# The first layer's gate product as seven block products of half size, with sums of weights on GpSimd

## The chip, the cores and the metric

The kernel runs on one core of a Trainium2 chip. What counts is the device time of one execution in microseconds. An engine's name stands as in the profile: PE is TensorE (PEld its weight loads), DVE is VectorE, ACT is ScalarE, POOL is GpSimd, SP is SyncE, which issues nearly all transfers.

## What is computed

Two layers act on 1024 tokens of width 1024. Each layer is a mixer, an MLP and a gated per-layer embedding (PLE). The change is in the first layer's PLE and in the end of the MLP before it:

```python
gate = jax.nn.sigmoid(rms_norm(h, ln_ple[layer]) @ w_ple_gate[layer])   # 1024x1024 @ 1024x1024
h = h + (p[layer] @ w_ple_proj[layer]) * gate                           # 1024x256 @ 256x1024
```

All is float32.

## The kernel before

**Products.** A float32 operand is split in two parts, `hi` and `lo` (`split`, line 229: ScalarE copies `hi` with rounding, VectorE subtracts it). A product is three matmuls (`mm3`): hi·hi, hi·lo, lo·hi, added up in PSUM. Activations lie with the features on the partitions, in `acc[m][h]`: 8 tiles `m` of 128 features, 2 halves `h` of 512 tokens. Weights are the stationary operand (128x128), activations the moving one (128x512).

**Normalisation.** `put_h` writes gain times `acc` as hi and lo without the row scale. The scale `rb[h]` (one over the root mean square of each token) comes from a sum of squares (`add_square`), which `rms` adds over the partitions with small matmuls against a column of ones; GpSimd takes the power. With `far=True` the scale is written to DRAM and read back to all partitions; both transfers are issued by SyncE, which takes its queue in order.

**The PLE.** `ple` loops over the two token halves, over four pieces of 256 columns of the gate's weight and over the two tiles in each. Each of the 16 results is one sum over 8 tiles in PSUM, 24 matmuls. `close` follows one result behind: it multiplies by `rb`, takes tanh, makes the projection `pp` (six matmuls) in an `aux` bank, combines and adds into `acc`, stores `acc` in `h_dram`, and adds its square. After a half, `put_h` makes the next stage's operands. The gate's weight is thus loaded and split twice.

**Buffers.** Raw weights have 8 buffers (`RB`), split weights 12 (`WB`, six pairs). `tmp` has 4. The slots `c0` to `c13`, `A0` to `A5` and `B` are reused by name. PSUM has 8 banks: tags `mm`, `tr`, `aux`, `sc`, two each. `mm_ps` takes tags in turn from `T.wide`.

**Order.** The instructions of each engine run in a fixed order. The context that builds the program plans it with modelled times (`schedule_with_timeline_sim=True`), by the order of the text where several could go; waits come from what an instruction reads and writes. So a step's place in its engine's queue is planned, and its time is not.

**Around the change.** The MLP's second product ends with `product2(2)` and `product2(4)`, whose sums `add` puts into `acc`. Behind the PLE comes `attention`: projections of v and of the first head's q and k, half 0 first. Its weights are split with the low parts on GpSimd. The MLP and the second layer's PLE (`ple_out`) already use seven block products, with sums of weights on VectorE.

Of the kernel before, what the change touches and what calls it, by code (L numbers as in the profile page):

```python
# [11 lines left out]
F32 = mybir.dt.float32  # L12
F32R = mybir.dt.float32r
# [5 lines left out]
P = 128  # L19
D = 1024  # L20
S = 1024
KT = D // P
# [21 lines left out]
def f32(ap):  # L44
    return ap.bitcast(F32)
# [73 lines left out]
class Trunk:  # L119
# [54 lines left out]
    def raw(self, n, m):  # L174
        return self.wp.tile([P, n, m], F32, tag="raw", name=self.nm("raw"), bufs=RB)

    def parts(self, raw, lo_engine):
        hi, lo = (self.wp.tile(list(raw.shape), F32R, tag="w", name=self.nm("w"), bufs=WB) for _ in range(2))
        self.split(raw, hi, lo, lo_engine)

        self.low_mark = self.split_mark
        return hi, lo
# [63 lines left out]
        nc.vector.scalar_tensor_tensor(lo, h, gain, f32(hi), ALU.mult, ALU.subtract)  # L246
        self.hs_new[half][k] = (hi, lo)

    def add_square(self, half, h):
        nc = self.nc  # L250
        if self.sqs[half] is None:
            self.sqs[half] = self.sp.tile([P, HT], F32, tag=f"sqs{half}", name=self.nm("sqs"), bufs=1)
            nc.scalar.activation(self.sqs[half], h, AF.Square)
        else:
            sq = self.tmp()
            nc.scalar.activation(sq, h, AF.Square)
            nc.vector.tensor_tensor(self.sqs[half], self.sqs[half], sq, ALU.add)

    def take_hs(self, half, ms=None, rows=True, far=False):

# [36 lines left out]
    def mlp(self, x, x_tags, gain, w1, w2, gain_next, h_dram, p, last):  # L297
# [319 lines left out]
        if last:  # L617
            product2(4, y, True)
            add(4, 1, y, put)
            x = [self.mm_ps() for _ in range(4)]  # L620
            product2(2, x, True, rms)
            self.mlp_mark = self.pe.mark
            add(0, 1, x, square)
        else:
            product2(2, y, True)
            add(0, 1, y, put)
            product2(4, x, False, rms)
            self.mlp_mark = self.pe.mark
            add(4, 1, x, put)
        self.hs[1] = self.hs_new[1]  # L630
        return acc, pT

# [25 lines left out]
        return hi, lo  # L658


    def ple(self, pT, acc, wg, wpj, gain_next, h_dram):
        nc = self.nc
        gates = []

        def close():
            h, m, ps = gates.pop(0)
            pp = self.aux_ps()
            for k in range(2):
                self.mm3(pp, [x[:, k, (m % 2) * P : (m % 2 + 1) * P] for x in wq[m // 2]], pT[h][k], k == 0, k == 1)
            t = self.tmp()  # L670
            nc.vector.tensor_tensor(t, ps, rb[h], ALU.mult)
            nc.scalar.activation(t, t, AF.Tanh, scale=0.5)
            t2 = self.tmp()
            nc.vector.scalar_tensor_tensor(t2, t, 1.0, pp, ALU.add, ALU.mult)
            nc.vector.scalar_tensor_tensor(acc[m][h], t2, 0.5, acc[m][h], ALU.mult, ALU.add)
            nc.sync.dma_start(h_dram[m, :, h * HT : (h + 1) * HT], acc[m][h])
            self.add_square(h, acc[m][h])

        hs, rb, sqs = list(self.hs), list(self.rb), self.sqs[1]
        self.new_hs()  # L680
        for h in range(2):
            for j in range(4):
                w = self.weight(wg[:, j * 256 : (j + 1) * 256], KT, 256)
                for ml in range(2):
                    m = 2 * j + ml
                    ps = self.mm_ps()
                    for k in range(KT):
                        self.mm3(ps, w.at(k, slice(ml * P, (ml + 1) * P)), hs[h][k], k == 0, k == KT - 1)
                    n = KT * h + m
                    if n == 0:  # L690
                        wq = [self.weight_p(wpj, i) for i in range(4)]
                    if n == 2:
                        rb[1] = self.rms(1, sqs, far=True)[1]
                    while len(gates) > (n < 3):
                        close()
                    gates.append((h, m, ps))
            close()
            for m in range(KT):
                self.put_h(m, h, acc[m][h], gain_next[:, m : m + 1])
            self.take_hs(h, rows=False)  # L700

# [1390 lines left out]
def trunk(tc, x, p, ln_mix_e, w_in_e, gmlp_v_gain, gmlp_ws, gmlp_bs, gdn_conv, gdn_a_log, gdn_dt_bias, gdn_out_gain,  # L2092
          w_out_e, ln_mix_o, w_qkv_o, attn_q_gain, attn_k_gain, diff_lambda, attn_sub_gain, w_out_o, ln_mlp, w_mlp1,
          w_mlp2, ln_ple, w_ple_gate, w_ple_proj, masks, out):
    with ExitStack() as ctx:
# [55 lines left out]
        for layer in range(2):  # L2151
            T.wide = ("mm", "tr")
            accs = [None] * 4

            def acc_of(m, h):
                i = 2 * h + m // 4
                if accs[i] is None:
                    accs[i] = T.slot(f"A{i}", [P, 4, HT], F32, "acc")
                return accs[i][:, m % 4]


            if layer:
# [12 lines left out]
            T.ple(pT, acc, w_ple_gate[0], w_ple_proj[0], gain[3], h_dram)  # L2175
            T.wide = ("mm",)
            T.attention(w_qkv_o[0], w_out_o[0], gain[4], h_dram)

# [40 lines left out]
```

## Time and profile before

| | us |
|---|---|
| median of 3 runs | 2503.58 (2502.16 to 2503.97) |
| profiled execution | 2502.4 |
| its span, first to last instruction | 2500.7 |
| PE busy in the span | 2490.9 |
| DVE busy | 1809.6 |
| ACT busy | 1312.8 |
| POOL busy | 284.0 |

In the rows of a timeline stand start, length, engine, line, operation, tiles (out<-in), shape, number, and in brackets the idle time before with what ended it. In a row of groups stand the number, the busy time, the mean length of one in ns, and the idle time before. Matmuls overlap, so their lengths are longer than the distance between two. In a row of waits: who waited, for whom, us in total, times, longest.

### The profile page before, as it was taken

Reading aid. Unit: us, or ns where it says so; the run is one execution under the profiler, and the core shown is the slowest. Engines: PE = TensorE matmul, PEld = TensorE weight load, DVE = VectorE, ACT = ScalarE, POOL = GpSimd, SP = SyncE. Lnnn points to the kernel's source line nnn. Section 1 sums busy time; section 2 is a strip of 40 time slices with the busy share of each in tenths; the row PEclk is TensorE's granted clock in tenths of the full one; section 3 lists DMA queues with packets and bytes.
Section 4 is the critical chain, followed back from the end, with each engine's and each line's share of the span. In section 5 each row is a group of like instructions: output and inputs, shape, how many; then the busy total and the mean of one; then the engine's idle time right before and its main releaser. Section 6 shows DMA issues by size and latency. Waiting matters only on the chain.

```text
span 2500.7 us, 39891 instructions
## 1 busy us (share of the span) xinstructions
PE 2490.9 (100%) x13905; PEld 2138.7 (86%) x13905; DVE 1809.6 (72%) x3542; ACT 1312.8 (52%) x2669; POOL 284.0 (11%) x267
## 2 busy tenths in 40 slices
PE   9999999999999999999999999999999999999999
PEld 7898998888888888888999999988888888888887
DVE  7868665787666887656577877776887666787586
ACT  6635473555555444544466666654654555445452
POOL 0211220000000000000444444410000000000000
PEclk9999999999999999999999999999999999999999
DMA  8464435467548756544211111367466548566651
GB/s 238 128 185 106 145 127 183 139 208 245 178 169 276 241 164 208 188 130 132 80 54 58 52 52 60 102 206 234 157 220 224 193 161 299 197 192 200 197 177 64
DMA packets 318834, 410.81 MB, mean 164 GB/s; under 512 B 45764, under 2 KB 181928, under 8 KB 318632
## 3 DMA queue, kind: packets, MB, share of 16 engines
q1 hardware_dynamic: 318072, 407.73, 50.9%
q8 instruction: 109, 1.79, 0.3%
q14 instruction: 93, 0.76, 0.1%
q10 hardware_dynamic: 560, 0.53, 0.1%
HBM read 295.95 MB, written 112.20 MB: 163 GB/s over the span
## 4 chain that ended last, share of the span: by engine, by line
PE 96%; DVE 2%; DMA 1%; issue 0%; ACT 0%; POOL 0%; SPq 0%; ACTq 0%; DVEq 0%
PE mm L80 83%; PE po L80 3%; PE qk L80 2%; PE aux L80 2%; PE tr L83 2%; DMA x<-in_x_dram 1%; DMA raw<-in_w_in_e_dram 0%; DVE lg L1128 0%; PE pks L80 0%; PE pkq L80 0%; PE pkk L80 0%; PE pvn L80 0%; PE pgm L80 0%; PE pab L83 0%; PE pst L80 0%
## 5 line engine op out<-in xcount | busy, mean ns | idle before, releaser
L230 ACT CAST w<-raw 128x512 fp32r<-128x512 f32 x598 | 366.5, 617 | 472.4 <-PE mm L80 410.2
L80 PE MATMUL mm<-g,w 128*128 128x512 f32 x2592 | 601.0, 394 | 0.0
L80 PEld LDWEIGHTS mm<-g,w 128*128 128x128 f32 x2592 | 486.9, 188 | 113.0
L80 PE MATMUL mm<-hi,w 128*128 128x512 f32 x1728 | 554.6, 396 | 0.1
L234 DVE TENSOR_TENSOR w<-raw,w 128x512 fp32r<-128x512 f32 x534 | 368.1, 696 | 199.3 <-ACT w L230 189.9
L80 PE MATMUL mm<-w,hi 128*128 128x256 f32 (+2 forms) x2528 | 507.4, 295 | 0.5 <-DVE k L1030 0.5
L80 PEld LDWEIGHTS mm<-w,hi 128*128 128x128 f32 x2528 | 401.2, 188 | 13.4 <-issue 0.7
L80 PEld LDWEIGHTS mm<-hi,w 128*128 128x128 f32 x1728 | 324.4, 188 | 74.7 <-DVE w L234 0.8
L80 PE MATMUL mm<-w,lo 128*128 128x256 f32 (+2 forms) x1264 | 370.2, 294 | 0.0
L80 PE MATMUL mm<-lo,w 128*128 128x512 f32 x864 | 340.3, 394 | 0.0
L80 PE MATMUL mm<-t,w 128*128 128x512 f32 x1152 | 271.2, 394 | 0.0
L80 PEld LDWEIGHTS mm<-t,w 128*128 128x128 f32 x1152 | 216.4, 188 | 50.5
L80 PEld LDWEIGHTS mm<-w,lo 128*128 128x128 f32 x1264 | 238.2, 189 | 5.5
L80 PEld LDWEIGHTS mm<-lo,w 128*128 128x128 f32 x864 | 162.5, 188 | 36.0
L275 POOL TENSOR_TENSOR r<-ms,mhalf 128x4 f32<-128x4 f32 x12 | 13.7, 1139 | 1512.3 <-DVE ms L273 1483.2
L234 DVE TENSOR_TENSOR g<-graw,g 128x512 fp32r<-128x512 f32 x216 | 148.0, 687 | 5.9 <-DMA gd<-g 5.0
L230 ACT CAST g<-graw 128x512 fp32r<-128x512 f32 x216 | 132.7, 617 | 22.7 <-DMA gd<-g 10.9
L1131 ACT ACTIVATE lg<-lg,nm 128x128 f32<-128x128 f32 (+7 forms) x128 | 99.2, 776 | 64.8 <-DVE nm L1128 62.9
L370 ACT ACTIVATE g<-g 128x512 f32<-128x512 f32 x100 | 63.0, 630 | 81.4 <-DVE g L304 81.0
L1128 DVE CUSTOM_DVE_ANT_0 lg<-qk,al 128x512 f32<-128x512 f32 (+3 forms) x128 | 74.4, 589 | 37.6 <-PE qk L80 33.6
L234 POOL TENSOR_TENSOR w<-raw,w 128x512 fp32r<-128x512 f32 x64 | 85.1, 1348 | 76.3 <-ACT w L230 51.5
L80 PE MATMUL mm<-ohi,w 128*128 128x512 f32 x256 | 83.6, 398 | 0.5 <-DVE t L1310 0.4
(360 smaller groups left out, 3573.9 us busy)
## 6 DMA issues: line engine op xcount, KB each, us to landing
raw<-in_w_mlp_dram SPq DMA_DIRECT2D x352, 256.0 KB, 3.4
graw<-gd SPq DMA_DIRECT2D x224, 256.0 KB, 2.8
gd<-g SPq DMA_DIRECT2D x192, 256.0 KB, 3.4
raw<-in_w_ple_gate_dram SPq DMA_DIRECT2D x76, 256.0 KB, 3.5
acc<-h_dram SPq DMA_DIRECT2D x64, 256.0 KB, 4.5
keep<-in_w_mlp_dram SPq DMA_DIRECT2D x64, 256.0 KB, 4.4
raw<-in_w_in_e_dram SPq DMA_DIRECT2D x60, 256.0 KB, 4.0
h_dram<-acc SPq DMA_DIRECT2D x48, 256.0 KB, 2.8
```

The lines of the kernel that those rows point to most:

```text
L80: self._next(self.engine.matmul(*a, **k))
L83: self._next(self.engine.transpose(*a, **k))
L230: inst = self.nc.scalar.copy(hi, src)
L234: inst = (lo_engine or self.nc.vector).tensor_tensor(lo, src, f32(hi), ALU.subtract)
L275: nc.gpsimd.tensor_tensor(r, ms, self.mhalf[:, 0:4], ALU.pow)
L370: nc.scalar.activation(g, src, AF.Relu)
L1128: nc.vector.tensor_tensor_reduce(out=lg[:, k0:k1], in0=ps[:, : k1 - k0], in1=al[:, u0 + k0 : u0 + k1], scale=-1.0, scalar=3.0e38 if c == 0 ...
L1131: nc.scalar.activation(lg[:, :n], lg[:, :n], AF.Exp, bias=nm[:, r, nch - 1 : nch], scale=-1.0, accum_out=me.sums[:, b, r : r + 1])
```

## The change

The gate product becomes seven products of half size (Strassen's scheme in Winograd's form). The weight is cut in four blocks by halves of outputs (`i`) and inputs (`j`), the activations by halves of features and tokens. Each block product is 4 x 4 tile products over 512 tokens. In the order of the text they are numbered 1 to 7. Products 1, 4, 5 and 6 (`chain`) are added up in the same four PSUM banks `x`, which are read after each of them. Products 2, 3 and 7 (`single`) go tile by tile through other banks. The sums of weights (`sum1`, `sum3`, `sum4`) are made on GpSimd; one of them goes to DRAM (`s2_dram`) and is read twice. One product has its weight's low part on GpSimd. The sums of activations (`t1` to `t4`) are made with the gain on VectorE and ScalarE; `t1` beside the MLP's last product, and the MLP no longer makes `put`'s operands for half 1. The additions of squares go to GpSimd. `close` runs for four results at a time, with products 2 and 7 and after products 5 and 6, and the projection's weights are loaded in two parts.

```diff
-    def add_square(self, half, h):
+    def add_square(self, half, h, eng=None):
...
-            nc.vector.tensor_tensor(self.sqs[half], self.sqs[half], sq, ALU.add)
+            (eng or nc.vector).tensor_tensor(self.sqs[half], self.sqs[half], sq, ALU.add)
...
             product2(2, y, True)
-            add(0, 1, y, put)
-            product2(4, x, False, rms)
+            add(0, 1, y, square)
+            t1 = self.hs_new[1]
+
+            def make_t1():
+                for k in range(4):
+                    z = self.scaled(self.tmp(), acc[k][0], gain_next[:, k : k + 1])
+                    nc.vector.scalar_tensor_tensor(z, acc[k][1], gain_next[:, k : k + 1], z, ALU.mult, ALU.subtract)
+                    t1[k] = self.split(z, *self.hs_parts(1, k))
+
+            product2(4, x, False, {**rms, 9: make_t1})
             self.mlp_mark = self.pe.mark
-            add(4, 1, x, put)
+            add(4, 1, x, lambda m, h: self.add_square(h, acc[m][h], nc.gpsimd))
...
+    def ple(self, pT, acc, gain, wg, wpj, gain_next, h_dram):
+        hs, rb, sqs = list(self.hs), list(self.rb), self.sqs[1]
+        b11, b21, t1 = hs[0][0:4], hs[0][4:], hs[1][0:4]
+        self.new_hs()
+        s2_dram = self.dp.tile([4, P, HT], F32, name="s2_dram")
...
+        def raw(i, j, k):
+            t = self.raw(1, HT)[:, 0]
+            nc.sync.dma_start(t, wg[(4 * j + k) * P : (4 * j + k + 1) * P, i * HT : (i + 1) * HT])
+            return t
...
+        def left(src, eng=nc.vector):
+            hi, lo = (self.wp.tile([P, 1, HT], F32R, tag="w", name=self.nm("w"), bufs=WB)[:, 0] for _ in range(2))
+            return self.split(src, hi, lo, eng)
...
+        def chain(ps, make, b, new=False):
+            for k in R:
+                a = make(k)
+                for q in R:
+                    one(ps[q], a, b[k], q, k, new and k == 0, k == 3, not new)
+
+        def single(a, b, tags, done):
+            for q in R:
+                ps = self.aux([P, HT], tags[q], "mm")
+                for k in R:
+                    one(ps, a[k], b[k], q, k, k == 0, k == 3, False)
+                done(q, ps)
+
+        def close(l, h, q, ps, plus, wp):
+            m = 4 * l + q
+            t = self.tmp()
+            if plus is not None:
+                tt(t, ps, plus, ALU.add)
+                ps = t
+            tt(t, ps, rb[h], ALU.mult)
+            nc.scalar.activation(t, t, AF.Tanh, scale=0.5)
             pp = self.aux_ps()
             for k in range(2):
+                self.mm3(pp, [x[:, q * P : (q + 1) * P] for x in wp[k]], pT[h][k], k == 0, k == 1)
+            nc.vector.scalar_tensor_tensor(t, t, 1.0, pp, ALU.add, ALU.mult)
+            a = stt(acc[m][h], t, 0.5, acc[m][h], ALU.add)
+            nc.sync.dma_start(h_dram[m, :, h * HT : (h + 1) * HT], a)
+            self.add_square(h, a, nc.gpsimd)
...
+        x = [self.mm_ps() for _ in R]
+        chain(x, lambda k: left(raw(0, 0, k)), b11, True)
+        a12 = [left(raw(0, 1, k)) for k in R]
+        u0 = f32_tiles((6, 7, 8, 9), "u")
+        for q in R:
+            nc.scalar.copy(u0[q], x[q])
...
+        for k in R:
+            self.scaled(t3[k], acc[k][1], g(k))
+            stt(t3[k], acc[4 + k][1], g(4 + k), t3[k], ALU.subtract)
+            stt(t2[k], acc[k][0], g(k), t3[k], ALU.add)
+        rb[1] = self.rms(1, sqs, far=True)[1]
+        single(a12, b21, ("sc",) * 4, lambda q, ps: close(0, 0, q, ps, u0[q], wp0))
+
+        def sum1(k):
+            a21, a22, a11 = raw(1, 0, k), raw(1, 1, k), raw(0, 0, k)
+            tt(a21, a21, a22, ALU.add, nc.gpsimd)
+            tt(a11, a21, a11, ALU.subtract, nc.gpsimd)
+            nc.sync.dma_start(s2_dram[k], a11)
+            return left(a21)
+
+        p5 = f32_tiles((6, 7, 8, 9), "p5")
+        s1 = [sum1(k) for k in R]
+        t2s = parts(t2, (0, 0))
+        single(s1, t1, ("sc",) * 4, lambda q, ps: nc.scalar.copy(p5[q], ps))
+        t3s = parts(t3, (0, 4))
+        b22 = put(1, 1, (1, 4), gain)
+        for k in R:
+            stt(t2[k], acc[4 + k][0], g(4 + k), t2[k], ALU.subtract)
+        chain(x, lambda k: left(sum2(k), nc.vector), t2s)
+        u = f32_tiles((10, 11, 12, 13), "u")
+        for q in R:
+            nc.scalar.copy(u[q], x[q])
+        t4s = parts(t2, (1, 0))
+
+        def sum3(k):
+            a11, a21 = raw(0, 0, k), raw(1, 0, k)
+            return left(tt(a11, a11, a21, ALU.subtract, nc.gpsimd), nc.vector)
+
+        chain(x, sum3, t3s)
+        wp1 = weight_p(1, [self.slot(f"c{i}", [P, HT], F32R, "wp") for i in range(4)])
+        for q in R:
+            close(1, 1, q, x[q], p5[q], wp1)
+        put_next(0, 0, (0, 0))
+        chain(x, lambda k: left(raw(1, 1, k), nc.gpsimd), t4s)
+        for q in R:
+            tt(u[q], u[q], p5[q], ALU.add, nc.gpsimd)
+        for q in R:
+            close(1, 0, q, x[q], None, wp1)
+
+        def sum4(k):
+            a12, s2 = raw(0, 1, k), sum2(k)
+            return left(tt(a12, a12, s2, ALU.subtract, nc.gpsimd), nc.vector)
+
+        put_next(1, 0, (1, 0))
+        single([sum4(k) for k in R], b22, ("sc", "sc", "tr", "tr"), lambda q, ps: close(0, 1, q, ps, u[q], wp0))
+        self.take_hs(0, rows=False)
+        put_next(1, 1, (0, 4))
+        put_next(0, 1, (1, 4))
+        self.take_hs(1, rows=False)
```

`sum2(k)` reads one saved sum back from `s2_dram` into a raw buffer; `parts` splits four activations; `put` and `put_next` are `put_h` for four tiles into given places.

More of the change, by code (lines that the diff above doesn't have):

```diff
@@ L667, in close @@
             pp = self.aux_ps()
             for k in range(2):
[L669 to L700, printed above, removed]
+                self.mm3(pp, [x[:, q * P : (q + 1) * P] for x in wp[k]], pT[h][k], k == 0, k == 1)
@@ new lines, in close, with put @@
+            nc.vector.scalar_tensor_tensor(t, t, 1.0, pp, ALU.add, ALU.mult)
+            a = stt(acc[m][h], t, 0.5, acc[m][h], ALU.add)
+            nc.sync.dma_start(h_dram[m, :, h * HT : (h + 1) * HT], a)
+            self.add_square(h, a, nc.gpsimd)
+        def put(l, h, place, by):
+            new = []
+            for q in R:
+                m = 4 * l + q
+                hi, lo = self.hs_parts(place[0], place[1] + q)
+                self.scaled(hi, acc[m][h], by[:, m : m + 1])
+                stt(lo, acc[m][h], by[:, m : m + 1], f32(hi), ALU.subtract)
+                new.append((hi, lo))
+            return new
@@ new lines, in put_next, with parts @@
+        def put_next(l, h, place):
+            self.hs_new[h][4 * l : 4 * l + 4] = put(l, h, place, gain_next)
+        def parts(srcs, place):
+            return [self.split(s, *self.hs_parts(place[0], place[1] + k)) for k, s in enumerate(srcs)]
+        x = [self.mm_ps() for _ in R]
[4 more added lines that the diff above has]
+            nc.scalar.copy(u0[q], x[q])
@@ L2174, in trunk @@
                 break
-            T.ple(pT, acc, w_ple_gate[0], w_ple_proj[0], gain[3], h_dram)
+            T.ple(pT, acc, gain[2], w_ple_gate[0], w_ple_proj[0], gain[3], h_dram)
             T.wide = ("mm",)
```

35 lines of the change are left out of this document (31 added, 4 removed).

## The prediction

> **What bounds the kernel now.** I read the page first: the engines, then the chain that ended last.
>
> ```profile
> span 2500.7 us, 39891 instructions
> PE 2490.9 (100%) x13905; PEld 2138.7 (86%) x13905; DVE 1809.6 (72%) x3542; ACT 1312.8 (52%) x2669; POOL 284.0 (11%) x267
> PE 96%; DVE 2%; DMA 1%; issue 0%; ACT 0%; POOL 0%; SPq 0%; ACTq 0%; DVEq 0%
> ```
>
> TensorE is the bound, and the last chain is nearly all matmul. Averages say nothing of this stage, so I cut the first layer's PLE out with the timeline and asked for busy times by window.
>
> ```profile
> 1091.50 0.40 PE L80 MATMUL mm<-hi,w 128*128 128x512 f32 x1
> ...
> 1204.16 0.39 PE L80 MATMUL aux<-phi,wpl 128*128 128x512 f32 x1
> 1204.39 0.40 PE L80 MATMUL mm<-w,hi 128*128 128x256 f32 x2
> ...
> 1213.01 0.95 PE L80 MATMUL aux<-ones,sqs 128*128 128x1 f32 x8
> ```
>
> ```profile
> core 0: us, PE busy (x) PEld busy (x) DVE busy (x) ACT busy (x) POOL busy (x), PEclk, DMA share, GB/s
> 1091.50:1204.39 112.89, 112.89 (x497) 92.04 (x496) 73.02 (x114) 50.44 (x87) 8.37 (x7) 1.00 0.38 119
> ...
> 2420.00:2450.00 30.00, 30.00 (x135) 24.43 (x134) 29.56 (x48) 17.40 (x32) 0.00 (x0) 1.00 0.17 57
> ```
>
> The PLE runs from 1091.50 to 1204.39, and TensorE has no gap in it, at clock 1.00. So a matmul taken out is worth its full pitch, and every wait that is put in is paid in full. VectorE has 39.9 us free, ScalarE 62, GpSimd 104. The last row is the second layer's PLE, which already has seven products with the sums on VectorE: there VectorE is busy 29.56 of 30.00 us and TensorE still has no gap. A full VectorE alone is thus no loss; a late one is. Now the groups of the stage.
>
> ```profile
> L80 PE MATMUL mm<-hi,w 128*128 128x512 f32 x256 | 82.1, 394 | 0.0
> L80 PE MATMUL mm<-lo,w 128*128 128x512 f32 x128 | 50.5, 394 | 0.0
> L230 ACT CAST w<-raw 128x512 fp32r<-128x512 f32 x33 | 20.1, 614 | 29.4 <-PE mm L80 25.3 <-DMA raw<-in_w_ple_gate_dram 3.9
> L234 DVE TENSOR_TENSOR w<-raw,w 128x512 fp32r<-128x512 f32 x27 | 18.4, 690 | 6.9 <-ACT w L230 6.6
> L80 PE MATMUL aux<-phi,wph 128*128 128x512 f32 x32 | 12.8, 399 | 0.0
> L257 DVE TENSOR_TENSOR sqs<-sqs,t 128x512 f32<-128x512 f32 x16 | 11.0, 688 | 0.6 <-ACT t L256 0.2
> L674 DVE SCALAR_TENSOR_TENSOR t<-t,aux 128x512 f32<-128x512 f32 x15 | 10.3, 686 | 24.2 <-PE aux L80 24.1
> L80 PE MATMUL aux<-ones,sqs 128*128 128x1 f32 x16 | 1.9, 239 | 0.0
> ```
>
> **Matmuls.** The gate product is 384 matmuls of 128x512 (256 + 128). The projection adds 96 (32, and twice more through the two other terms of `mm3`). Two sums of squares take 1.9 us. The pitch is (112.89 - 1.9) / 480 = 0.231 us; the 394 ns of one overlaps its neighbours and is not the price. Seven block products of 4 x 4 tile products, three matmuls each, are 7 x 48 = 336. The projection stays at 16 x 6. So 48 go: 48 x 0.231 = **11.1 us less**, and the stage becomes 101.8 us if TensorE never waits. Sums in PSUM cost no matmul: the chained products only clear the start flag.
>
> **Loads.** Instead of 32 pieces of the gate's weight come 44 and four reads of a saved sum; four sums are stored. That is 20 transfers of 256 KB more, 5 MB on some 13 MB (119 GB/s x 112.89 us), with the DMA engines 0.38 busy.
>
> ```profile
> raw<-in_w_ple_gate_dram SPq DMA_DIRECT2D x76, 256.0 KB, 3.5
> ...
> ACT w L230 <- DMA raw<-in_w_ple_gate_dram: 3.9, 1, 3.9
> ...
> SPq L281 <- DMA rd<-r: 16.8, 2, 8.5
> ```
>
> The whole stage waited for a weight once, 3.9 us on ScalarE, with eight raw buffers covering it. What threatens is the queue: SyncE waits up to 8.5 us in `rms(far=True)` for the row scale to come back, and what is behind it stands. In the new order that wait falls behind product 1 (some 14 to 23 us into the stage). Queued behind it are stores of the saved sums and perhaps the last pieces for product 3. These sums are read for product 4, at 40 us; the pieces are wanted at 31. A load issued at 23, 3.5 us to landing, 1.3 of sum (GpSimd's rows below) and 1.3 of split (0.61 and 0.69) is ready at 29. I take nothing, with 3 us as the upper end.
>
> **VectorE and GpSimd.** Counted from the diff, VectorE has these 128x512 operations from the first matmul on: 28 splits of weights less the 4 of product 1 that come earlier and 4 given to GpSimd, 4 splits of the projection, 12 of activations, 16 combinations with the gain (t2, t3, b22, t4), 60 in `close` (12 have the added sum, 48 the rest), 16 `put`: 128, where the window's row counts 114. The additions of squares go to GpSimd, which also gets 16 sums, 4 low parts and 4 additions of u and p5; with the four squares at the end of the MLP it has 42 (two of the PLE's squares are plain writes by ScalarE). The rows that price both lie at the end of the stage, where GpSimd already splits attention weights.
>
> ```profile
> 1198.27 1.35 POOL L234 TENSOR_TENSOR w<-raw,w 128x512 fp32r<-128x512 f32 x1 [8.59 <-ACT w L230]
> 1200.54 1.43 POOL L234 TENSOR_TENSOR w<-raw,w 128x512 fp32r<-128x512 f32 x1 [0.91 <-ACT w L230]
> 1203.42 3.29 POOL L234 TENSOR_TENSOR w<-raw,w 128x512 fp32r<-128x512 f32 x2 [1.46 <-ACT w L230]
> ...
> 1215.31 5.04 POOL L234 TENSOR_TENSOR w<-raw,w 128x512 fp32r<-128x512 f32 x4
> ```
>
> ```profile
> 1197.71 0.75 DVE L246 SCALAR_TENSOR_TENSOR lo<-acc,cols,hi 128x512 fp32r<-128x512 f32 x1
> 1198.38 0.68 DVE L671 TENSOR_TENSOR t<-mm,rb 128x512 f32<-128x512 f32 x1
> 1198.98 1.19 DVE L246 SCALAR_TENSOR_TENSOR lo<-acc,cols,hi 128x512 fp32r<-128x512 f32 x1
> 1200.10 0.68 DVE L257 TENSOR_TENSOR sqs<-sqs,t 128x512 f32<-128x512 f32 x1
> 1200.70 3.13 DVE L246 SCALAR_TENSOR_TENSOR lo<-acc,cols,hi 128x512 fp32r<-128x512 f32 x3
> 1203.76 0.68 DVE L674 SCALAR_TENSOR_TENSOR t<-t,aux 128x512 f32<-128x512 f32 x1
> 1204.36 1.19 DVE L246 SCALAR_TENSOR_TENSOR lo<-acc,cols,hi 128x512 fp32r<-128x512 f32 x1
> 1205.47 1.79 DVE L675 SCALAR_TENSOR_TENSOR acc<-t,acc 128x512 f32<-128x512 f32 x1
> ...
> 1211.35 0.69 DVE L257 TENSOR_TENSOR sqs<-sqs,t 128x512 f32<-128x512 f32 x1 [0.70 <-ACT t L256]
> ```
>
> Starts 1197.71, 1198.38 and 1198.98 give VectorE's pitch: 0.67 us with a gain column, 0.60 without. Thirty-two have one: 32 x 0.67 + 96 x 0.60 = 79 us of 101.8, which fits. An undisturbed GpSimd operation is 5.04 / 4 = 1.26 us, so its 42 are 53 us, which fits too. But the rows also show the two in each other's way. With GpSimd at work, an operation with two SBUF inputs takes 1.19 or 1.79 us instead of 0.75 and 0.69, and three take 3.13 instead of some 2.09; the two that read PSUM (`mm`, `aux`) keep 0.68. The loss is 0.44 + 1.04 + 0.44 + 1.10 = 3.0 us for four GpSimd operations, 0.76 each; GpSimd loses 6.07 - 5.04 = 1.0 us. Of VectorE's 128 only 32 read PSUM (12 additions, 4 multiplications, 16 with the projection). At 0.76 the 42 cost 32 us: 79 + 32 = 111, over 101.8. So VectorE will be late in places.
>
> [...]
>
> Where does lateness reach TensorE? I laid the new order out from 0 at the first matmul: product 1 to 11; sum of squares; product 2 with its four closings to 29; product 3 to 40; the two middle chained products to 62; closings to 68; product 6 to 79; closings to 84; product 7 with closings to 101.8. From 40 to 62 VectorE has about 14 operations (9 us): lateness is made up there, and those GpSimd operations cost nothing. Three places have little cover:
> - At 29. Of the 12 `w` buffers, product 2 holds 8 to its last quarter, so two of product 3's four splits start 2 us before it ends and are wanted 3 us after. In product 2 VectorE has 24 operations, 15 us, and some 11 of GpSimd (8 us): 23 in 17, less a lead of about 3. Slack after the split itself is 3.6. Cost 0 to 3, taken as 1.
> - At 79. Four banks are finished together; the third projection needs an `aux` buffer that VectorE frees by the first closing, about half a microsecond ahead. Lateness of 1 to 2 us comes through: 0 to 5, taken as 1. The same at 62, but VectorE arrives rested.
> - The end. Before, the last square ended at 1212.04 and TensorE's sum of squares stood at 1213.01 between attention matmuls, 8.6 us past the stage. Its place in the new order is planned; where VectorE or GpSimd is later than planned, TensorE stands there: 0 to 6, taken as 1. Half 1 itself is read later still.
>
> Tags `mm` and `tr`, taken four at once, need two banks of the MLP's last sums, 1.4 us later than the first two: nothing. ScalarE gets twelve copies from PSUM and some twenty scalings; with 50.44 of 112.89 us busy it hides them; without that cover they would cost at most their length at the same three places. The four t1 operands go beside the MLP's last product, where four `put`s leave: nothing.
>
> **Sum.** 2502.4 (profiled execution) - 11.1 + 3 = 2494.3. The median stands 1.2 above that execution, so the forecast is **2495.5**.
>
> **The rivals.** (a) VectorE's lateness is half absorbed: the 3.6 us of slack at 29 and the half microsecond at 79 go to a backlog near the computed 111 - 101.8 = 9 us. Waits of 9 us give 2503.6 - 11.1 + 9 = 2501.5, no difference. For it: the sum of 111. Against: 22 us in the middle are idle. (b) Slower: two-input operations and GpSimd exclude each other for whole instructions, and VectorE becomes the bound. Each of 42 costs it 1.26, so 79 + 53 = 132 us; 8 of that may run past the stage, as in the trace (1204.39 to 1212.04); waits are 132 - 8 - 101.8 = 22 us: 2503.6 - 11.1 + 22 = 2514.5. Its place is the closings from 62 on and the end. It decides slower from 16 us of waits, (16 + 101.8 + 8 - 79) / 42 = 1.1 us for each GpSimd operation, against 0.76 seen. For it: 1.79 and 3.13. Against: those rows stand in a stretch without idle VectorE time. (c) SyncE's waits hold product 3's weights: 3 to 5 us more on the forecast, about 2499.5. Against: the stage's single wait of 3.9. (d) All is hidden: 2492.5. That the matmuls do not go can't be: their count follows from the loops.
>
> **How the numbers follow.** A measurement of this kernel can tell 0.2%, 5 us, from no change: 2498.6 and 2508.6. Forecast (waits to 6 us) with (d): 0.50. (a) and (c): 0.22, of which 0.04 still lands below 2498.6. (b), from 2508.6 on: 0.28. Faster 0.54, same 0.18, slower 0.28. The forecast's own range is 2492 to 2498.5; to leave no more than 2 in 10 out the range goes to 2512.
>
> **What would show it.** Right: 432 matmuls of 128x512 in the stage at the same pitch, TensorE's gaps together about 3 us, at product 3's start, in the closings after product 6, at the last sum of squares, each released by VectorE or GpSimd; 128x512 operations of two SBUF inputs stretched to 1.2 to 1.9 us. Wrong: gaps over 11 us, a longer pitch or clock below 1.00, or gaps released by a DMA.

## The result, and the profile after

| | before | after |
|---|---|---|
| median of 6 runs, us | 2503.18 (2502.16 to 2503.97) | 2514.04 (2511.77 to 2516.18) |
| profiled execution, us | 2502.4 | 2515.1 |
| its span, us | 2500.7 | 2513.3 |

The kernel became slower: the ratio is 1.0042 with a 95% interval of 1.0031 to 1.0053. The forecast of 2495.5 us was wrong in its sign, and 2514.04 lies above its range.

The page after, with the same lines as were read before:

```profile
PE 2491.7 (99%) x13857; PEld 2136.2 (85%) x13857; DVE 1846.4 (73%) x3556; ACT 1327.5 (53%) x2697; POOL 351.2 (14%) x309
PE 93%; DVE 4%; issue 1%; DMA 1%; ACT 1%; POOL 0%; SPq 0%; DVEq 0%; ACTq 0%; POOLq 0%
```

13905 - 13857 = 48 matmuls are gone, as counted. The last chain now runs over VectorE for 4% instead of 2%. How much of this belongs to the stage is told by an instruction that both kernels have behind it, the first `qk` matmul of the attention. The busy times from the first matmul of the PLE to that instruction, before:

```profile
1091.50:1244.77 153.27, 153.27 (x841) 132.41 (x840) 91.40 (x144) 65.17 (x114) 28.64 (x25) 1.00 0.34 106
```

The row of after, and below it the stage in parts (columns as in the prediction's windows: PE, PEld, DVE, ACT, POOL, granted clock, DMA share, GB/s):

```profile
1091.38:1253.56 162.18, 150.96 (x792) 127.70 (x791) 127.32 (x157) 74.59 (x133) 96.21 (x69) 0.96 0.41 127
...
1100.00:1110.00 10.00, 6.75 (x28) 5.52 (x27) 10.00 (x7) 1.86 (x4) 9.92 (x7) 0.83 0.34 113
1110.00:1120.00 10.00, 7.94 (x25) 5.79 (x24) 10.00 (x15) 3.11 (x6) 2.82 (x3) 0.66 0.47 151
1120.00:1180.00 60.00, 59.98 (x259) 48.30 (x259) 49.53 (x61) 31.64 (x56) 31.41 (x22) 1.00 0.55 163
1180.00:1224.00 44.00, 38.76 (x221) 32.44 (x219) 39.04 (x46) 22.50 (x41) 27.50 (x20) 1.00 0.31 102
1224.00:1230.00 6.00, 5.35 (x32) 5.27 (x33) 0.55 (x4) 1.08 (x3) 5.50 (x5) 0.72 0.49 138
```

The stretch takes 162.18 us instead of 153.27, 8.9 more, where 11.1 less were expected: **20.0 us are lost in it**. TensorE stands for 162.18 - 150.96 = 11.2 us. The other 8.8 are in its busy time: 150.96, where 153.27 - 11.1 = 142.2 would do. The clock column names a part of that, 0.83, 0.66 and 0.72 in three rows where it was 1.00 before. From the `qk` matmul to the end it is 2513.3 - 1253.56 = 1259.7 us, where it was 2500.7 - 1244.77 = 1255.9: 3.8 more are lost behind the stage.

The loss has two places, the stage's start and its end. From 1120 to 1180 TensorE has no gap and VectorE is idle for 10.5 of 60 us: the middle is as forecast. Before it, from 1100 to 1120, VectorE is busy without a pause (10.00 and 10.00) and TensorE is not. Who released TensorE tells the view of its waits, 1085 to 1250:

```profile
PE aux L80 <- DVE t L751: 3.7, 4, 1.6
PE mm L80 <- DVE w L234: 3.3, 2, 2.1
PE aux L80 <- POOL sqs L257: 3.2, 1, 3.2
PE mm L80 <- POOL w L234: 0.6, 1, 0.6
PE mm L80 <- ACT v L1178: 0.3, 1, 0.3
```

No DMA is among them. But for 0.3 us, for which an attention matmul waits for ScalarE, all are VectorE's or GpSimd's. TensorE's timeline shows the places:

```profile
1103.71 0.40 PE L80 MATMUL mm<-hi,w 128*128 128x512 f32 x1
1107.35 1.87 PE L80 MATMUL aux<-ones,sqs 128*128 128x1 f32 x8 [3.25 <-POOL sqs L257]
...
1110.08 0.63 PE L80 MATMUL aux<-phi,wp 128*128 128x512 f32 x1
1110.51 0.63 PE L80 MATMUL aux<-plo,wp 128*128 128x512 f32 x1
1113.19 1.22 PE L80 MATMUL mm<-hi,w 128*128 128x512 f32 x2 [2.06 <-DVE w L234]
...
1204.74 0.50 PE L80 MATMUL aux<-phi,wp 128*128 128x512 f32 x1 [1.63 <-DVE t L751]
```

The longest gap is where product 1 ends, 13 us into the stage: the sum of squares for the row scale waits 3.25 us for GpSimd. A few matmuls later a weight of product 2 is not split yet, 2.06 us. Of the others, 1.24 us is a split for product 7, and 1.63 and 1.33 us are closings of product 7; the rest are below 0.7 us each. After the first gap two matmuls stand 1110.51 - 1110.08 = 0.43 us apart, nearly twice the 0.231 of before.

Why are both engines late there? VectorE's timeline of after, in the first stretch:

```profile
1097.61 1.78 DVE L691 SCALAR_TENSOR_TENSOR lo<-acc,cols,hi 128x512 fp32r<-128x512 f32 x1
1099.31 1.79 DVE L234 TENSOR_TENSOR w<-raw,w 128x512 fp32r<-128x512 f32 x1
1101.03 3.48 DVE L691 SCALAR_TENSOR_TENSOR t<-acc,cols,t 128x512 f32<-128x512 f32 x2
...
1112.46 0.68 DVE L234 TENSOR_TENSOR w<-raw,w 128x512 fp32r<-128x512 f32 x1
```

and GpSimd's:

```profile
1091.80 3.01 POOL L687 TENSOR_TENSOR raw<-raw,raw 128x512 f32<-128x512 f32 x2 [26.24 <-DVE w L234]
...
1097.09 1.75 POOL L257 TENSOR_TENSOR sqs<-sqs,t 128x512 f32<-128x512 f32 x1
1098.80 1.75 POOL L687 TENSOR_TENSOR raw<-raw,raw 128x512 f32<-128x512 f32 x1
1100.51 1.74 POOL L257 TENSOR_TENSOR sqs<-sqs,t 128x512 f32<-128x512 f32 x1
...
1107.26 3.40 POOL L687 TENSOR_TENSOR raw<-raw,raw 128x512 f32<-128x512 f32 x2
```

The two engines go in step, one operation of each in 1.71 us (1097.09, 1098.80, 1100.51 on one, 1097.61, 1099.31, 1101.03 on the other). Alone a split takes VectorE 0.68 us, as at 1112.46, when GpSimd is done. From 1091.80 to 1110.66 GpSimd has eleven such operations, seven of the eight first sums of weights and the four squares of the MLP's end, beside product 1 and the gap behind it. And the groups of the stage (1091.38 to 1224), for VectorE and for GpSimd:

```profile
L691 DVE SCALAR_TENSOR_TENSOR lo<-acc,cols,hi 128x512 fp32r<-128x512 f32 x20 | 30.2, 1513 | 4.2 <-ACT hi L670 4.1
L234 DVE TENSOR_TENSOR w<-raw,w 128x512 fp32r<-128x512 f32 x20 | 19.7, 984 | 9.3 <-ACT w L230 9.3
L691 DVE SCALAR_TENSOR_TENSOR acc<-t,acc 128x512 f32<-128x512 f32 x16 | 16.2, 1014 | 0.4
L691 DVE SCALAR_TENSOR_TENSOR t<-acc,cols,t 128x512 f32<-128x512 f32 x12 | 13.4, 1131 | 0.0
L751 DVE SCALAR_TENSOR_TENSOR t<-t,aux 128x512 f32<-128x512 f32 x16 | 10.8, 676 | 0.8 <-ACT t L747 0.7
L687 DVE TENSOR_TENSOR t<-t,rb 128x512 f32<-128x512 f32 x12 | 10.5, 877 | 0.3
```

```profile
L257 POOL TENSOR_TENSOR sqs<-sqs,t 128x512 f32<-128x512 f32 x18 | 27.8, 1542 | 22.2 <-ACT t L256 22.1
L687 POOL TENSOR_TENSOR raw<-raw,raw 128x512 f32<-128x512 f32 x16 | 24.5, 1535 | 45.9 <-DVE w L234 26.2 <-DMA raw<-in_w_ple_gate_dram 17.7 <-DMA raw<-s_dram 1.5
```

Against 750 ns with a gain column and 690 ns without, the operations with two SBUF inputs lose 20 x 0.763 + 20 x 0.294 + 16 x 0.324 + 12 x 0.381 + 12 x 0.187 = 33.2 us; the one that reads PSUM (`aux`) loses nothing (676 ns, 686 before). GpSimd has 49 operations of this size in that window: 18 squares, 16 sums, 4 additions of `u` and `p5`, and 11 low parts of weights.

### The profile page after: what moved, and what is told of

Its sections match the earlier page's. It is cut to its first block, busy times and chain, and to the rows that moved or that the text cites. A ratio compares the mean times of both kernels' runs of the same rounds, so it can differ in the third digit from the quotient of the medians.

```text
span 2513.3 us, 39935 instructions
## 1 busy us (share of the span) xinstructions
PE 2491.7 (99%) x13857; PEld 2136.2 (85%) x13857; DVE 1846.4 (73%) x3556; ACT 1327.5 (53%) x2697; POOL 351.2 (14%) x309
## 3 DMA queue, kind: packets, MB, share of 16 engines
q8 instruction: 109, 1.79, 0.3%
## 4 chain that ended last, share of the span: by engine, by line
PE 93%; DVE 4%; issue 1%; DMA 1%; ACT 1%; POOL 0%; SPq 0%; DVEq 0%; ACTq 0%; POOLq 0%
PE mm L80 80%; PE po L80 3%; PE qk L80 2%; PE tr L83 2%; PE aux L80 2%; DVE acc L691 0%; DMA rd<-r 0%; DVE lo L691 0%; DVE t L691 0%; DVE lg L1261 0%; PE aux L83 0%; DMA raw<-in_w_ple_gate_dram 0%; DVE w L234 0%; DVE t L751 0%; PE pks L80 0%
## 5 line engine op out<-in xcount | busy, mean ns | idle before, releaser
L230 ACT CAST w<-raw 128x512 fp32r<-128x512 f32 (+1 forms) x594 | 363.5, 618 | 431.2 <-PE mm L80 378.1
L80 PE MATMUL mm<-hi,w 128*128 128x512 f32 x1696 | 545.7, 397 | 3.3 <-DVE w L234 3.3
L234 DVE TENSOR_TENSOR w<-raw,w 128x512 fp32r<-128x512 f32 (+1 forms) x526 | 365.5, 701 | 192.8 <-ACT w L230 184.4
L80 PEld LDWEIGHTS mm<-hi,w 128*128 128x128 f32 x1696 | 318.9, 188 | 77.7 <-DVE w L234 4.9
L80 PE MATMUL mm<-lo,w 128*128 128x512 f32 x848 | 334.4, 395 | 0.0
L234 DVE TENSOR_TENSOR g<-graw,g 128x512 fp32r<-128x512 f32 x216 | 147.6, 685 | 5.3 <-DMA gd<-g 4.2
L1264 ACT ACTIVATE lg<-lg,nm 128x256 f32<-128x256 f32 (+7 forms) x128 | 99.2, 775 | 70.3 <-DVE nm L1261 68.4
L234 POOL TENSOR_TENSOR w<-raw,w 128x512 fp32r<-128x512 f32 x68 | 91.5, 1366 | 42.5 <-ACT w L230 24.1
```

What stands on the lines that cost most here:

```text
L80: self._next(self.engine.matmul(*a, **k))
L230: inst = self.nc.scalar.copy(hi, src)
L234: inst = (lo_engine or self.nc.vector).tensor_tensor(lo, src, f32(hi), ALU.subtract)
L1264: nc.scalar.activation(lg[:, :n], lg[:, :n], AF.Exp, bias=nm[:, r, nch - 1 : nch], scale=-1.0, accum_out=me.sums[:, b, r : r + 1])
```

## The experiments

My theory was that GpSimd's operations make VectorE (and themselves) late at the stage's start and end, by excluding each other. The expectations call it the port theory; the name is a label of mine, and what makes the two engines exclude each other no run shows. Rivals: that the sum of squares stands too early in the order and holds up what is behind it; that VectorE simply has too much to do, with or without GpSimd; that work which nobody yet wants lies ahead of urgent work. Medians of before, in the four groups of runs, were 2503.35 to 2503.69 us.

**1. The sum of squares behind product 2.**

```diff
-        rb[1] = self.rms(1, sqs, far=True)[1]
         single(a12, b21, ("sc",) * 4, lambda q, ps: close(0, 0, q, ps, u0[q], wp0))
+        rb[1] = self.rms(1, sqs, far=True)[1]
```

> The changed kernel (2514.0) with one call moved: the sum of squares of half 1 (rms) stands after product 2 instead of before it. Port theory (VectorE operations with two SBUF inputs and GpSimd operations shut each other out, so both run late): TensorE's 3.3 us wait for the squares at 1103.7 goes, and the slow clock behind it; the 2.1 us wait for product 2's late split and the waits in the closings stay: 2508 to 2511. Queue theory (GpSimd is only slow and has the sums queued in front of the squares; nothing else is late): the wait and nearly all of the loss at 1100 to 1120 (some 9 us) go: 2505 to 2507.

2514.1 us, ratio 1.0041 (1.0026 to 1.0056): nothing gained, and both numbers missed. The longest of TensorE's waits in this kernel is 6.4 us, for a split of VectorE (`w`, L234). The wait went from the sum of squares to the next thing that VectorE owed, the split for product 2, and the two early gaps became one. The place of the sum alone is not the cause.

**2. The sums of weights on VectorE.** The 16 sums, the 4 low parts and the 4 additions of `u` and `p5`; GpSimd keeps the squares.

```diff
-            tt(a21, a21, a22, ALU.add, nc.gpsimd)
-            tt(a11, a21, a11, ALU.subtract, nc.gpsimd)
+            tt(a21, a21, a22, ALU.add)
+            tt(a11, a21, a11, ALU.subtract)
...
```

> The changed kernel with the 16 sums of weights, the 4 low parts and the 4 additions of u and p5 on VectorE; the squares stay on GpSimd. VectorE has 152 operations instead of 128 (93 us of 101.8), GpSimd 18 instead of 42. Port theory: faster, since 24 shut-outs go: 2500 to 2507. Queue theory (VectorE is late because it has too much of its own): slower than or like the changed kernel, 2514 to 2522.

2520.14 us, 1.0069 (1.0052 to 1.0086): 6 us worse still, where my theory had expected a gain; it is the range of the rival, by which VectorE has too much to do of its own. TensorE waits 11.6 us for VectorE at two of the closings' operations (`t`, L687), 8.3 us at one of them. Each operation taken from GpSimd costs VectorE 0.6 to 0.7 us of its own, about what it cost as a neighbour (33.2 us for the 49 GpSimd operations in the window is 0.68 each).

**3. Everything on VectorE.** Experiment 2, and the squares as well (`self.add_square(h, a)`).

> The changed kernel with nothing on GpSimd but the powers and the attention weights, as before the change: sums and squares on VectorE, 170 operations there, 105 us in a stage of 101.8 plus some 8 after it. Port theory: faster than the changed kernel and than the kernel before: 2493 to 2500. Queue theory: VectorE is overfull and TensorE waits in the closings: 2505 to 2515.

2522.4 us, 1.0074 (1.0059 to 1.0089), slower than either number. The stage's window:

```profile
1091.60:1230.00 138.40, 121.96 (x553) 99.96 (x551) 118.67 (x177) 67.44 (x119) 20.90 (x14) 0.93 0.44 139
```

VectorE is busy for 118.67 us, as after the change (117.19 to 1224), now with 42 more instructions of its own and little excess (`lo` x20 at 939 ns where it was 1513, the splits at 732 where they were 984). So seven products on VectorE alone are slower too: its own work fills it as the exclusion did.

**4. GpSimd busy, but reading nothing.** Each of the 38 additions (sums of weights, `u` and `p5`, squares) becomes two instructions that only write; these sums are thus left out of the result.

```diff
-            eng.tensor_tensor(out, a, b, op)
+            if eng is nc.gpsimd:
+                for _ in range(2):
+                    eng.iota(out, pattern=[[1, HT]], base=1, channel_multiplier=1, ...)
```

> The changed kernel with each sum and each square's addition on GpSimd replaced by two iotas of the same size, which write SBUF and read nothing, so that GpSimd has some 1 us of work at each place (the four low parts stay as they are); sums and squares are left out of the result. Port theory: VectorE's operations with two SBUF inputs return to 0.69 and 0.75 us from 1.7 to 1.8, and most of the 20 us that TensorE loses goes: 2494 to 2501. Queue theory: GpSimd is as busy and as late: 2509 to 2515.

2499.75 us, 0.9981 (0.9971 to 0.9990), **14.3 us less** than with the additions. The window of the stage, then the two waits that TensorE has left:

```profile
1092.50:1207.00 114.50, 111.92 (x529) 92.17 (x528) 88.58 (x133) 62.28 (x110) 56.49 (x87) 1.00 0.50 160
```

```profile
PE aux L80 <- ACT wp L230: 1.6, 1, 1.6
PE mm L80 <- ACT u L814: 1.0, 1, 1.0
```

GpSimd is still busy for 56.49 us (two of 0.56 for an addition of 1.26), in the same place in the order, and the clock is 1.00. VectorE's timeline has the order of after at the same place:

```profile
1096.32 0.75 DVE L699 SCALAR_TENSOR_TENSOR lo<-acc,cols,hi 128x512 fp32r<-128x512 f32 x1
1096.98 0.68 DVE L234 TENSOR_TENSOR w<-raw,w 128x512 fp32r<-128x512 f32 x1
...
1100.23 1.40 DVE L699 SCALAR_TENSOR_TENSOR lo<-acc,cols,hi 128x512 fp32r<-128x512 f32 x2
```

and GpSimd's:

```profile
1095.10 1.58 POOL L693 IOTA raw<- 128x512 f32 x3 [0.93 <-DMA raw<-in_w_ple_gate_dram]
1096.63 0.56 POOL L259 IOTA t<- 128x512 f32 x1
...
1100.52 1.59 POOL L259 IOTA t<- 128x512 f32 x3
```

1.78 and 1.79 us have become 0.75 and 0.68, and two combinations with the gain take 1.40 instead of 3.48, beside GpSimd's writes. So VectorE was stretched beside the additions, which read two tiles, and not beside the writes. Not all of the 14.3 us need be VectorE's: nobody adds the squares now, so the sum of squares behind product 1, after's first gap, no longer waits for GpSimd. Experiment 1, where that wait went and nothing was gained, speaks against a large share of that wait alone, but does not rule one out.

**5. The squares alone back on VectorE.** `self.add_square(h, a)`, and `square` at the end of the MLP.

> The changed kernel with the squares' additions back on VectorE (18 of them), the sums still on GpSimd: VectorE has 146 operations (90 us), GpSimd 24. With sums on VectorE instead the time was 2520.1, with both 2522.4, with GpSimd reading nothing 2499.8: so neither sharing the work nor sparing GpSimd was enough. Port theory with a full VectorE: 18 shut-outs (each some 1.1 us) are exchanged for 18 operations of 0.6 us, so a little faster than the changed kernel: 2507 to 2514. Pure queue theory (the squares stood behind the sums on GpSimd, and only that held TensorE): the wait at the first sum of squares goes altogether, 2504 to 2507.

2510.46 us, 1.0029 (1.0018 to 1.0041). It holds the range expected, and is the best version that computes everything, 7 us above before. What is left of the waits at the start is 4.1 us for the split for product 2.

**6. The kernel before, with the PLE's squares on GpSimd.** The other way round: exclusion, but room to spare.

```diff
-            self.add_square(h, acc[m][h])
+            self.add_square(h, acc[m][h], nc.gpsimd)
```

> The kernel before with one part of the change alone: the additions of squares in its PLE on GpSimd. VectorE has 40 us to spare there. Port theory: two-input operations on VectorE beside them are stretched, but the spare time takes it up until the end of the stage, where the last square is later by about 1.3 to 3 us: 2503 to 2507. A rival, that any GpSimd work here costs its whole length on the path: 14 x 1.26 = 18 us, 2515 to 2521.

2503.78 us, 1.0002 (0.9992 to 1.0011), no difference. The stage:

```profile
1091.50:1204.39 112.89, 112.89 (x497) 92.06 (x497) 69.11 (x100) 50.24 (x87) 24.98 (x19) 1.00 0.36 117
```

Fourteen additions left VectorE and 3.9 us came off its busy time (73.02 before), not 14 x 0.688 = 9.6: the rest, 5.7 us or 0.4 for each, went to the exclusion. With VectorE idle for 44 us TensorE does not wait. Here the exclusion costs no time, as VectorE has some to spare.

**7. Work that is not urgent, later.** The operands `b22`, wanted only by product 7, and the sums `t2`, `t3` are planned from 1092 to 1112, ahead of the split that product 2 waits for. Here `b22` is planned behind product 4, and the scalings for `t3` and `t2` behind product 1. This is an order for the plan; nothing in the run waits for it.

```diff
-            self.scaled(t3[k], acc[k][1], g(k))
+            self.pe.behind(nc.scalar.activation(t3[k], acc[k][1], AF.Copy, scale=g(k)), mark1)
...
-        b22 = put(1, 1, (1, 4), gain)
...
         chain(x, lambda k: left(sum2(k), nc.vector), t2s)
+        b22 = put(1, 1, (1, 4), gain, self.pe.mark)
```

> The changed kernel with the same operations, of which sixteen are held back in the planned order: the 4 low parts of b22, wanted only for product 7, stand behind product 4, and the 8 combinations t3 and t2 behind product 1 (scalings on ScalarE with them). In the trace of the changed kernel they stand at 1092 to 1112 in front of the split that TensorE waits for, 1.7 us each. Theory (shut-outs stretch operations that are not urgent, and the fixed order makes the urgent ones wait behind them): the loss of 9 us at 1100 to 1120 falls to 2 to 4, the rest stays: 2507 to 2510. Rival (VectorE and GpSimd together are simply too full from 12 to 35 us into the stage, in whatever order): the wait moves to product 3 or 4, 2512 to 2517.

2511.68 us, 1.0036 (1.0023 to 1.0049): between the two numbers. TensorE still waits 3.8 us for `sqs` and 4.2 for the closings. VectorE's timeline shows that the edit did only part of what it was meant to do:

```profile
1099.67 10.22 DVE L691 SCALAR_TENSOR_TENSOR t<-acc,cols,t 128x512 f32<-128x512 f32 x6
```

Six of the eight combinations still run ahead of a split for product 2 (at 1109.82), 1.7 us each beside GpSimd's sums and squares. So this run does not decide between the two.

**8. TensorE kept at work in the first gap.** Fifteen matmuls into a bank that nobody reads, ahead of the sum of squares, ask whether the low clock follows from standing idle.

```diff
+        idle = self.aux([P, HT], "sc", "idle")
+        for _ in range(5):
+            one(idle, hs[0][4], hs[0][4], 0, 0, True, True, False)
         rb[1] = self.rms(1, sqs, far=True)[1]
```

> The changed kernel with 15 matmuls of 128x512 in a bank that nobody reads in front of the first sum of squares (3.5 us, as long as TensorE's wait there). If the clock of 0.66 that stands behind that wait follows from TensorE's idleness, it stays at 1.00 and the slow pitch (0.43 instead of 0.23 us at 1109 to 1117, some 4 us) goes at no other cost: 2509 to 2511. If the clock falls for another reason, or the wait grows by the matmuls: 2514 to 2518.

2512.16 us, 1.0038 (1.0024 to 1.0052), between the two numbers; against after the difference of 1.9 is within the spread of both. The windows around the gap:

```profile
1103.00:1111.00 8.00, 6.28 (x32) 4.88 (x30) 8.00 (x6) 1.14 (x2) 7.92 (x6) 1.00 0.35 112
...
1116.40:1122.00 5.60, 5.60 (x13) 4.44 (x14) 5.60 (x11) 0.00 (x0) 0.52 (x1) 0.50 0.56 176
```

With the gap filled down to 1.72 us the clock stays at 1.00 to 1111. Then VectorE, no earlier than before, leaves TensorE idle for 2.85 and 1.33 us, and the clock is 0.50. So at this place the low clock stood behind gaps, of 3.25 us in after and of 2.85 and 1.33 here, and not behind the first gap when it was 1.72; I take it as their consequence and not as a cause of its own.

**9 to 11. Room at the start.** In these three, `t3` and `t2` are planned behind the second tile of product 2 and `b22` behind product 4; `t2` is thereby made from `acc` after product 2's closings have changed it, so that these kernels compute something else. 9 has all squares on VectorE, 10 only the MLP's four, 11 is 9 with one `put` of the next stage planned behind product 7.

```diff
+        single(a12, b21, ("sc",) * 4, done2)
         t3, t2 = f32_tiles((10, 11, 12, 13), "t3"), f32_tiles((0, 1, 2, 3), "t2")
...
+            self.pe.behind(nc.scalar.activation(t3[k], acc[k][1], AF.Copy, scale=g(k)), marks[1])
...
-            self.add_square(h, a, nc.gpsimd)
+            self.add_square(h, a)
```

> The kernel with the squares on VectorE (2510.5), and twelve VectorE combinations held back further than in the run that held them behind product 1: t3 and t2 behind the second tile of product 2, the low parts of b22 behind product 4. GpSimd's sums for product 3 then meet hardly any VectorE work from 1092 to 1108. Theory (shut-outs hurt where the sums of GpSimd and operations that are not urgent lie in one stretch of the plan, so that the urgent split and the squares wait): the loss of 9 us at 1100 to 1120 falls under 3, and some of it comes back at product 4, as t2 is wanted there: 2500 to 2505. Rival (the work of both is too much for the first 40 us, in whatever order): 2508 to 2514.

2512.15 us, 1.0039 (1.0025 to 1.0053). Windows of experiment 9:

```profile
1100.00:1120.00 20.00, 20.00 (x93) 16.37 (x92) 16.65 (x23) 10.48 (x19) 7.49 (x5) 1.00 0.53 155
1110.00:1150.00 40.00, 36.34 (x147) 27.79 (x146) 39.80 (x57) 23.78 (x43) 8.85 (x6) 0.96 0.58 150
```

The early loss is gone: no gap from 1100 to 1120. But VectorE is then busy for 39.80 of 40 us, and at 1140 to 1150 TensorE is at work for 6.42 of 10 us. The loss was moved, not removed, and the time is in the range of the rival, that the work of both is too much in whatever order.

> As the run with the squares on VectorE and t3, t2, b22 held back, but only the MLP's four squares are on VectorE; the closings' 14 stay on GpSimd. Theory: the early loss falls as there, and the closings at 1180 to 1225 lose their 6 to 9 us as in the changed kernel: 2504 to 2509. Rival (too full in whatever order): 2510 to 2515.

2511.61 us, 1.0031 (1.0019 to 1.0043), again the rival's range, with one wait that is longer than any of after: 6.8 us for a split of the projection's weights on VectorE.

> As the run with the squares on VectorE and t3, t2, b22 held back, with the four low parts of put_next(1, 1) also held back behind product 7, where they stood between the last closings' operations. Theory: the last closings wait less for VectorE, 1 to 3 us off: 2498 to 2503. Rival (half 1's operands and squares then come too late for attention, or the closings do not wait for these): no difference from that run.

2513.0 us, 1.0038 (1.0023 to 1.0053), no difference from 9, as the rival had it; moving the `put` at the end gave nothing.

**12. Only the squares read nothing.** As experiment 4, but for the 18 additions of squares alone; the squares are left out.

> The changed kernel with only the 18 additions of squares on GpSimd replaced by two iotas each, which read nothing; the sums of weights, the low parts and the additions of u and p5 stay as they are (the squares are left out of the result). In the changed kernel VectorE's two-input operations lost 33 us beside GpSimd; with all of it reading nothing the time was 2499.8, 14 us less. If each shut-out counts alike wherever it falls: 18 of 42, some 6 us less, 2508. If what counts is the room at the two ends (at 1100 to 1120, where four squares meet eight sums, and at the closings from 1180, where GpSimd has squares and attention weights alone): the loss in the closings goes and the early one about halves, 2502 to 2506.

2503.31 us, 0.9998 (0.9988 to 1.0008), in the second of the two ranges. Of the 14.3 us of experiment 4, 2514.04 - 2503.31 = 10.7 come with the 18 squares and 3.6 with the 20 others, each within some 2 us by the spread of the runs. The number of operations would give 18 / 38 x 14.3 = 6.8 for the squares. The squares lie at product 1's end and beside the closings, which TensorE waits for; of the sums half lie in the middle, where VectorE has room. But the squares also carry the wait of the row scale, so this run can't tell their place from that wait. The longest wait left is that for the first closing of product 2. Ahead of its addition VectorE has combinations with the gain for `t2` and `t3`, of which three are stretched to 1.8 us beside sums of weights:

```profile
1116.08 0.68 DVE L691 TENSOR_TENSOR t<-mm,u 128x512 f32<-128x512 f32 x1
...
1116.81 0.80 PE L80 MATMUL mm<-hi,w 128*128 128x512 f32 x1 [3.58 <-DVE t L691]
```

## Why the prediction was wrong

**Matmuls: right.** 48 went, at 0.231 us where the clock was 1.00 (59.98 us / 259 = 0.2316 from 1120 to 1180). 11.1 us were there to be had.

**Exclusion: right in size.** 32 us were estimated and 33.2 measured, on operations with two SBUF inputs only. By the operation it is 0.68 us instead of 0.76, for the 49 GpSimd operations in the window to 1224 (seven of them low parts of attention weights) where 42 were counted.

**SyncE and the loads: right.** None of TensorE's gaps in the stage was released by a DMA. The count was off: the page has 80 loads of the gate's weight (`raw<-in_w_ple_gate_dram`) instead of 76, so the stage has 36 pieces and not 44; with eight reads of the saved sums and four stores that is 16 transfers more, not 20. No term rested on it.

**The middle: right.** The two middle chained products have no gap, and VectorE's lateness ends there.

**The step that failed is "lateness to TensorE's waits", 1 + 1 + 1 us.** It was 20.0 us up to the `qk` matmul, 11.2 of gaps and 8.8 in the busy time, and 3.8 behind it: 2502.4 - 11.1 + 20.0 + 3.8 = 2515.1. Three things were wrong in it.
- *The place.* The first place that I named was product 3's start, at 29 us, and nothing waited there. The loss was at 13 and 20 us, where product 1 ends and product 2 begins. Product 1 was not laid out against VectorE and GpSimd at all: I set some 11 GpSimd operations against product 2, and the plan has eleven beside product 1 and the gap behind it. At that density the mean of 0.76 does not hold: one operation of each takes 1.71 us, so each of GpSimd's costs VectorE 1.71 - 0.67 = 1.04 us, and eleven such steps are 19 us, where product 1 lasts 12.7 (1091.38 to 1104.1). The closings after product 6 made no wait; behind them a split for product 7 came 1.24 us late. From 1200 on the gaps are 4.6 us, where 1 was taken, and mostly not where I named them: the last sum of squares waits 0.56 us, two closings of product 7 wait 1.63 and 1.33.
- *The clock.* I wrote "clock below 1.00" as a sign of being wrong, without a price. After two of the gaps the matmuls ran at a granted clock of 0.50: from 1107.35 to 1116.8 and from 1226 to 1229. Eight small matmuls (1.73 us to the next instead of some 0.9), twelve of 128x512 at 0.43 instead of 0.23 and 3 us in the second stretch make about 5 of the 8.8 us. The other 4, by the starts of the matmuls against the mean distances of before, are an estimate: 2.0 us at the gaps, where the distance of two matmuls is some 0.2 us more than gap and pitch, 0.9 in the matmuls right behind a gap (0.33 instead of 0.23 us to the next), and 1.1 spread over the rest.
- *Behind the stage* 3.8 us more were lost, which I had not counted. The largest part stands in one place of the trace, where a later row scale comes late, which before does not wait for:

```profile
1767.94 1.35 PE L80 MATMUL aux<-ident,r 128*128 128x128 f32 x8 [2.09 <-POOL r L275]
```

  Behind it the clock is at 0.50 for 3.41 us, which is some 1.7 us more. In experiment 4, with hardly any exclusion, the same wait is 2.43 us, and 3.5 are lost behind the stage as well (2497.9 - 1238.47 = 1259.4); in experiment 11 it is 0.65, and nothing is lost (1255.8). What makes this wait long in some of the kernels stays open.

**Rival (b) gave 2514.5, but for another reason, so its number was luck.** Its mechanism, every GpSimd operation shutting VectorE out for its full 1.26 us until VectorE is the bound, was a supposition and did not happen: the mean is 0.68, below the 1.1 from which it was to decide, and VectorE is idle for 10.5 of 60 us in the middle. What is true of it is local: in the first 20 us the price is 1.04 and VectorE is never idle. Taken for every pair, 1.26 us overstates the stage; taken as the mean of a stretch with room, my 0.76 understated its start. Experiment 4 shows that the loss goes with GpSimd's additions, which read: with writes in their place the kernel is 3.8 us faster than before. How much of that is VectorE's stretched work and how much the wait of the row scale for GpSimd's own additions, experiments 4 and 12 do not separate. Why these are 3.8 and not 11.1 is known in part: 3.5 behind the stage and 2.6 in two waits for ScalarE. Experiments 2 and 3 show that VectorE alone is worse, and 9 to 11 that these other orders only move the loss: near the stage's start VectorE has too much to do, whether by its own work or by the exclusion.

## What to carry to other kernels

Where a saving on the bound engine is paid for with work on others, lay that work out in time from the first instruction of the stage, not as a sum over the stage: the exclusion cost nothing in the middle of this stage and nothing in a kernel whose VectorE had room, and up to 14 us where it had none. An operation of 128x512 moved from VectorE to GpSimd was little relief where all inputs lie in SBUF: of 0.69 us moved, 0.4 (experiment 6) to nearly all (the change) were lost again. And a gap of TensorE of 3.25 us cost more than its length here: the clock was back at 1.00 only 9.5 us behind its end.

## What the runs showed of the hardware

- Excluding each other costs both: in after, from 1097 to 1111, one operation of each takes 1.71 us, little less than 0.67 + 1.26 = 1.93 us, so that they hardly overlap; GpSimd's mean goes from 1.26 (before, undisturbed) to 1.54 us. In experiment 4 instructions of GpSimd that only write (0.56 us each) leave VectorE's at 0.68 and 0.75.
- Up to the `qk` matmul the granted clock of after fell to 0.50 twice, for 10.24 and for 3.41 us (3.41 us is called a step below). The rows, divided at its changes:

```profile
1103.17:1106.58 3.41, 0.93 (x4) 0.40 (x3) 3.41 (x3) 1.14 (x2) 3.33 (x3) 1.00 0.51 159
1106.58:1116.82 10.24, 7.41 (x21) 5.72 (x22) 10.24 (x11) 3.11 (x6) 5.56 (x4) 0.50 0.34 107
...
1222.64:1226.05 3.41, 2.76 (x22) 2.39 (x21) 1.19 (x2) 2.44 (x6) 3.41 (x4) 1.00 0.04 10
1226.05:1229.46 3.41, 3.41 (x19) 3.41 (x18) 0.00 (x0) 0.00 (x0) 3.41 (x3) 0.50 0.76 210
```

  With a third low stretch from 1768.77 to 1772.18 they are three, one and one steps long, and the second and third begin 35.0 and 194.0 steps behind the first. The length of a gap alone did not tell whether the clock fell: ahead of 1226.05 the longest is 0.65 us, beside eight matmuls of one column, while in after a gap of 1.63 us (ahead of 1204.74) and in experiment 8 one of 1.72 us left it at 1.00. An estimate from the matmuls' columns (0.231 us for 512) fits better: in the trace of after they fill 0.22, 0.37 and 0.22 of the step ahead of the three falls, and 0.44 or more of every other step at 1.00 between 1000 and 2490 us.
